# Where a token tile is transposed in the long sequence's first pass of an encoder layer

## The chip, the cores and the metric

The kernel runs on one core of a Trainium2 chip. The metric is the device time of one execution in microseconds (us). A core has five engines that run side by side, each with its own queue in order: TensorE (PE, matmuls and transposes), VectorE (DVE), ScalarE (ACT), GpSimd (POOL) and SyncE (SP, which here only issues DMAs).

## The reference

One layer of an encoder over two sequences, a short one of 512 tokens (`x_sample`) and a long one of 1024 (`x_prompt`), both of width 1024, and a final norm:

```
xn = RMSNorm(x)
z  = xn @ W_in  -> [q_A | k_A | v_A | q_B | k_B | v_B | gate_A | gate_B]
branch A: grouped-query attention (8 heads, 2 key/value heads of 64),
          q and k RMS-normalised per head, 2-D rotary
branch B: neighbourhood attention, 8 heads
mix = (sigmoid(gate_A) * (o_A @ W_pA) + sigmoid(gate_B) * (o_B @ W_pB)) @ W_out
x = x + mix
x = x + relu(RMSNorm(x) @ W_up)^2 @ W_down
```

All arrays are float32.

## The kernel before

Every float32 operand of a matmul is held as a high part (`fp32r`, written by ACT as a rounding copy) and a low part (written by DVE as source minus high part), and every product is three matmuls, high by high, high by low and low by high (`mm3`, lines 191 to 193). The short sequence goes through the token mixer first (`Trunk(0, ...)`), then the long one (`Trunk(1, ...)`); the two-matrix part of both sequences follows at the end.

`run` is the token mixer of one sequence. Its first loop, `for g in range(2)`, goes over the two key/value groups of branch A; within it `for tt in range(NT)` goes over the tiles of 128 tokens, 8 of them for the long sequence. The pass with `g == 0` is called the first pass here. In its step `tt` PE computes

- `z`, the tile's 384 columns of q, k and v (24 matmuls of 128x384, an accumulation over the 1024 rows of `W_in`),
- `values(tt - 2)`, 256 columns of branch B's values for the tile two steps back (24 matmuls of 128x256, `zvs`),
- `heads_t(tt - 2)`, three transposes of that tile's normed and rotated heads (`pqs`).

All of them read the normed tile transposed, so that the width lies along the partitions. Such a tile is made in four steps. `stat` squares the loaded tile `xt` on ACT and gets its root mean square by way of DVE (`ms_s`) and POOL (`rs_s`, a power); `scale` multiplies on DVE by that and by the norm's weights (`xns`, line 378); `p0_t` calls `transpose_tile`, which transposes the eight 128x128 blocks on PE into a PSUM tile of two banks (`ptxs`, line 275; there are two such buffers, `pbig`, shared with `pqs`), copies its halves on ACT into the high part (`xs_1h`, line 285) and subtracts them on DVE for the low part (`xs_1l`, line 291). Of the long sequence, tiles 0 to 3 are transposed while the short sequence is being finished (`ready` is then 4, and so is `r0`); tiles 4 to 7 are loaded, normed and transposed in the first pass itself (`fresh and not first`). `xs_1h` and `xs_1l` are the transposed tiles 4 to 7.

After `z` of a tile come its head norm and rotation: five squares on ACT (`sqs`), the mean on DVE (`ms_As`), the power on POOL (`rs_As`, line 176), five scalings on DVE (`ts`, line 657), two products on POOL (`us`) and the rest on DVE. DVE's queue stands still between `ms_As` and `ts` unless something is put between them.

The order on each engine is made at build time: a scheduler takes the instructions by their estimated readiness, except those passed to `tc.keep_in_program_order`, which keep the order in which the code is written among each other. `transpose_tile` pins its ACT copies and DVE subtractions if `pin` is set; before, this holds for no tile of the long sequence. In the code before, step `tt` calls `next_tile`, the transpose of tile `tt + 1`, ahead of `z`:

```
to_come = fresh and tr.ready <= tt + 1 < NT
in_z = first and to_come and tt > 0
if to_come and not in_z:
    next_tile()
```

Squares of tiles 4, 5, 6 and 7 (`stat`) are written at the end of steps 0, 1, 3 and 4, the scaling in the next step, between `ms_As` and `ts`. Normed tiles 4 and 6 share a buffer, and 5 and 7; the loaded tiles have two buffers as well, and the load of tile 6 or 7 waits until tile 4 or 5 is scaled.

Of the kernel before, what the change touches and what calls it, by code (L numbers as in the profile page):

```python
# [21 lines left out]
HD = 64  # L22
# [39 lines left out]
def encoder(ctx: ExitStack, tc: tile.TileContext, xs, outs, w):  # L62
# [107 lines left out]
    def rstd(ss, n, width, name, pin=False):  # L170
        m = sml.tile([P, 8], F32, tag="ms", name=f"ms_{name}")
        op = nc.vector.tensor_scalar(m[:, :n], ss, 1.0 / width, EPS, op0=ALU.mult, op1=ALU.add)  # L172
        if pin:
            tc.keep_in_program_order(op)
        r = sml.tile([P, 8], F32, tag="rs", name=f"rs_{name}")
        nc.gpsimd.tensor_tensor(r[:, :n], m[:, :n], mhalf[:, :n], op=ALU.pow)  # L176
        return r
# [93 lines left out]
    def transpose_tile(xn, dest, j, nm, pin=False, between=()):  # L271

        pt = big(f"pt{nm}")
        for c in range(NC8):
            nc.tensor.transpose(pt[:, c * P : (c + 1) * P], xn[:, c * P : (c + 1) * P], ident)
        view = [
            (
                pt[:, q * 512 : (q + 1) * 512].rearrange("p (c t) -> p c t", t=P),
                dest[0][q][:, :, j * P : (j + 1) * P],
                dest[1][q][:, :, j * P : (j + 1) * P],  # L280
            )
            for q in range(2)
        ]
        for src, hi, lo in view:
            op = nc.scalar.activation(hi, src, AF.Copy)
            if pin:
                tc.keep_in_program_order(op)
        for i, (src, hi, lo) in enumerate(view):
            for step in between[i : i + 1]:
                step()  # L290
            op = nc.vector.tensor_tensor(lo, src, hi.bitcast(F32), op=ALU.subtract)
            if pin:
                tc.keep_in_program_order(op)
# [57 lines left out]
    class Trunk:  # L351
# [27 lines left out]
            tc.keep_in_program_order(op)  # L379
            return xn  # L380

        def p0_t(self, tt, xn, between=()):
            tb, j = divmod(tt, 4)
            if tb not in self.xhl:
                self.xhl[tb] = new_hl(f"x{self.N}_{tb}", (True, self.NB == 1 or tb == 1))
            transpose_tile(xn, self.xhl[tb], j, f"x{self.N}_{tt}", self.t0 + tt < 4, between)
            self.ready = tt + 1

        def xh(self, tb, c):
# [5 lines left out]
    def run(tr, nxt, first):  # L395
        N, x, T, NT, NB = tr.N, tr.x, tr.T, tr.NT, tr.NB
# [85 lines left out]
        for g in range(2):  # L482
            with phase(f"phR{N}_{g}") as ph:
                xn_of = {}
                fresh = g == 0 and tr.ready < NT
                if fresh and not first:
# [10 lines left out]
                    gb = gb[:, 0]  # L497
# [108 lines left out]
                for tt in range(NT):  # L606
# [5 lines left out]
                            xn_of[3] = tr.scale(st_of.pop(3), gb)  # L612
                        flush_heads()

                    to_come = fresh and tr.ready <= tt + 1 < NT
                    in_z = first and to_come and tt > 0
                    if to_come and not in_z:
                        next_tile()
# [27 lines left out]
                    ss = sml.tile([P, 8], F32, tag="ss", name=f"ssA{nm}")  # L646
                    for i in range(5):
                        nc.scalar.activation(sq[:, i, :], zq[:, i, :], AF.Square, accum_out=ss[:, i : i + 1])
                    r = rstd(ss[:, :5], 5, HD, f"A{nm}", fresh and (tt < 2 if first else bool(st_of)))
                    ahead_ = fresh and not first and bool(st_of)  # L650
                    for t_ in list(st_of) if ahead_ else []:
                        xn_of[t_] = tr.scale(st_of.pop(t_), gb)

                    def rotate(tt, nm, z, zq, r, rt, pin):
                        t = ph.tile([P, 5, HD], F32, tag="t", name=f"t{nm}", bufs=2)
# [27 lines left out]
                    heads.append(partial(rotate, tt, nm, z, zq, r, rt, first and fresh and tt < 2 or ahead_))  # L683
                    if not (first and fresh and tt < 2):
                        flush_heads()
                    t_ = {0: 4, 1: 5, 3: 6, 4: 7}.get(tt, NT) if fresh and not first else NT
                    if t_ < NT:
                        xn = xn_to.pop(t_, None)
                        if xn is None:
                            xn = ph.tile([P, D], F32, tag=f"xn{5 - t_ & 1}", name=f"xn{N}_{t_}", bufs=1)  # L690
                        st_of[t_] = tr.stat(t_, ph, xt_of.pop(t_), xn=xn)
# [1114 lines left out]
```

## Time and profile before

| | |
|---|---|
| median of 3 runs | 2143.0 us (2142.17 to 2143.53) |
| the profiled execution | 2141.17 us |
| its span, first to last instruction | 2139.3 us |
| PE busy | 2117.0 us, 99% of the span |
| DVE busy | 1472.7 us, 69% |
| ACT busy | 1115.0 us, 52% |
| POOL busy | 390.1 us, 18% |
| mean granted clock of TensorE | 0.998 of full speed |

The profile is of one execution. Its views used here are: the page with its totals; the waits (who waited for whom, in total and at longest); windows (busy time of each engine, granted clock and DMA load in a stretch that is chosen); and the timeline (each instruction with its start, its duration, and in brackets the idle time ahead of it and what ended it). A matmul's start and end overlap those of its neighbours, since PE works on several in a row; the distance from start to start is what a matmul costs. Times are counted from the start of the span. The first pass of the long sequence lies between 379 and 451 us.

### The profile page before, as it was taken

The page shows a single profiled execution, that of the slowest core. Times are in us where ns is not written, and L with a number is a line of the kernel's source. Part 1 is how long each engine was busy: PE and PEld are TensorE (multiplying, and loading weights), DVE is VectorE, ACT ScalarE, POOL GpSimd, SP SyncE. Part 2 cuts the span into 40 slices and gives each one's busy share as a digit, 9 for nine tenths or more (in the row PEclk, how much of TensorE's full clock was granted, in tenths as well). Part 3 has the DMA queues.
Part 4 walks back from the last instruction along what each step waited for, and adds up shares of the span by engine and source line. Part 5 has one row for each costly group of instructions (what it writes and reads, how often), then busy time and mean ns, then how long its engine had stood idle before and what let it go on. Part 6 is the DMA issues. An engine that isn't in the chain of part 4 may idle for free.

```text
span 2139.3 us, 31783 instructions
## 1 busy us (share of the span) xinstructions
PE 2117.0 (99%) x10970; PEld 1849.2 (86%) x10970; DVE 1472.7 (69%) x2802; ACT 1115.0 (52%) x2343; POOL 390.1 (18%) x506
## 2 busy tenths in 40 slices
PE   9999999999999999999999999999999999999998
PEld 8888878988898888888888999999999988888886
DVE  6675686777667754656782877778777777769563
ACT  5664564557546644655530666556655643434352
POOL 2232420433233214433300200003000000000000
PEclk9999999999999999999999999999999999999999
DMA  6435567620222132433462665578544799688561
GB/s 192 125 107 168 157 185 243 191 70 26 61 77 66 43 103 85 127 104 100 148 234 105 219 194 190 166 252 206 161 144 157 261 350 342 215 287 276 159 204 62
DMA packets 319578, 350.91 MB, mean 164 GB/s; under 512 B 31160, under 2 KB 255032, under 8 KB 319417
## 3 DMA queue, kind: packets, MB, share of 16 engines
q1 hardware_dynamic: 277927, 279.65, 41.5%
q10 hardware_dynamic: 35810, 52.19, 7.0%
q0 software_dynamic: 5680, 17.04, 2.9%
q8 instruction: 87, 1.43, 0.3%
q14 instruction: 74, 0.61, 0.1%
HBM read 264.85 MB, written 87.88 MB: 165 GB/s over the span
## 4 chain that ended last, share of the span: by engine, by line
PE 51%; DVE 1%; issue 0%; ACT 0%; POOL 0%; POOLq 0%; DVEq 0%
PE dn L191 6%; PE dn L193 6%; PE dn L192 6%; PE ud L192 2%; PE uc L192 2%; PE uc L191 2%; PE ud L191 2%; PE ud L193 2%; PE uc L193 2%; PE ua L192 2%; PE ua L191 2%; PE ua L193 2%; PE ops L191 1%; PE ops L192 1%; PE ops L193 1%; PE ub L192 1%
## 5 line engine op out<-in xcount | busy, mean ns | idle before, releaser
L193 PE MATMUL dn<-wd,al 128*128 128x512 f32 x624 | 242.8, 389 | 0.0
L192 PE MATMUL dn<-wd,ah 128*128 128x512 f32 x624 | 242.8, 389 | 0.0
L191 PE MATMUL dn<-wd,ah 128*128 128x512 f32 x624 | 242.7, 389 | 0.0
L1274 ACT ACTIVATE ah<-ar 128x512 fp32r<-128x512 f32 x168 | 104.7, 628 | 208.9 <-PE dn L192 190.9
L1275 DVE TENSOR_TENSOR al<-ar,ah 128x512 fp32r<-128x512 f32 x168 | 115.6, 694 | 75.3 <-ACT ah L1274 66.5
L193 PEld LDWEIGHTS dn<-wd,al 128*128 128x128 f32 x624 | 117.1, 188 | 24.5
L192 PEld LDWEIGHTS dn<-wd,ah 128*128 128x128 f32 x624 | 117.1, 188 | 24.2
L191 PEld LDWEIGHTS dn<-wd,ah 128*128 128x128 f32 x624 | 117.1, 188 | 24.2
L730 POOL TENSOR_SCALAR ps<-ps,rls 128x1024 f32<-128x1024 f32 (+1 forms) x96 | 96.8, 1009 | 215.5 <-DVE rls L729 201.2
L770 DVE TENSOR_TENSOR ptls<-pTs,pths 128x512 fp32r<-128x512 f32 x160 | 107.6, 686 | 37.8 <-ACT pths L769 37.1
L769 ACT ACTIVATE pths<-pTs 128x512 fp32r<-128x512 f32 x160 | 94.1, 598 | 74.0 <-PE pTs L764 71.8
L724 DVE TENSOR_REDUCE nms<-ss 128x1 f32<-128x1024 f32 (+1 forms) x96 | 99.9, 1041 | 25.5 <-PE ss L722 25.0
L176 POOL TENSOR_TENSOR rs_f<-ms_f,mhalf 128x1 f32<-128x1 f32 x6 | 4.0, 667 | 590.7 <-DVE ms_f L172 590.7
L191 PE MATMUL gpss<-xs_0h,w_gs 128*128 128x512 f32 x256 | 104.7, 409 | 0.3
L727 ACT ACTIVATE ps<-ss,nms 128x1024 f32<-128x1024 f32 (+1 forms) x96 | 93.2, 972 | 22.5 <-DVE nms L724 20.0
L764 PEld LDWEIGHTS pTs<-ident,ps 128*128 128x128 f32 x640 | 78.1, 140 | 28.3 <-POOL ps L730 4.2
L193 PE MATMUL gpss<-xs_0h,w_gs 128*128 128x512 f32 x256 | 100.9, 394 | 0.0
L192 PE MATMUL gpss<-xs_0l,w_gs 128*128 128x512 f32 x256 | 100.8, 394 | 0.0
L764 PE MATMUL pTs<-ident,ps 128*128 128x128 f32 x640 | 98.9, 274 | 1.3 <-DVE ptls L770 0.6
L1274 ACT ACTIVATE A<-S 128x512 fp32r<-128x512 f32 x128 | 76.1, 624 | 30.5 <-DVE S L1337 26.5
L1275 DVE TENSOR_TENSOR A<-S,A 128x512 fp32r<-128x512 f32 x128 | 84.5, 686 | 3.4 <-ACT A L1274 3.4
L1393 ACT ACTIVATE c<-c 128x384 f32<-128x384 f32 x97 | 50.8, 524 | 68.0 <-DVE c L1392 67.9
(332 smaller groups left out, 6400.6 us busy)
## 6 DMA issues: line engine op xcount, KB each, us to landing
ar<-ud SPq DMA_DIRECT2D x120, 512.0 KB
br<-in_w_mlp_down_dram SPq DMA_DIRECT2D x72, 512.0 KB
rawu<-in_w_mlp_up_dram SPq DMA_DIRECT2D x64, 512.0 KB
ud<-c ACTq DMA_DIRECT2D x128, 192.0 KB
raw_gs<-in_w_in_dram SPq DMA_DIRECT2D x32, 512.0 KB
zgs<-sgs ACTq DMA_DIRECT2D x48, 256.0 KB
ud<-cs SPq DMA_DIRECT2D x64, 192.0 KB
raw_os<-in_w_out_dram SPq DMA_DIRECT2D x16, 512.0 KB
```

The lines of the kernel that those rows point to most:

```text
L191: nc.tensor.matmul(out, ah, bh, start=start, stop=False, **kw)
L192: nc.tensor.matmul(out, ah, bl, start=False, stop=False, **kw)
L193: nc.tensor.matmul(out, al, bh, start=False, stop=stop, **kw)
L724: nc.vector.tensor_reduce(nm_, s, axis=AX.X, op=ALU.max, negate=True)
L727: nc.scalar.activation(p, s, AF.Exp, bias=nm_, accum_out=l)
L730: nc.gpsimd.tensor_scalar(p, p, rl, 1.0, op0=ALU.mult, op1=ALU.mult)
L764: nc.tensor.transpose(pt[:, j * P : (j + 1) * P], PP[u, j][:, kc * P : (kc + 1) * P], ident)
L769: nc.scalar.activation(hi, pt, AF.Copy)
L770: nc.vector.tensor_tensor(lo, pt, hi.bitcast(F32), op=ALU.subtract)
L1274: nc.scalar.activation(hi, src, AF.Copy)
L1275: nc.vector.tensor_tensor(lo, src, hi.bitcast(F32), op=ALU.subtract)
L1393: nc.scalar.activation(t, t, AF.Relu)
```

## The change

Three things change in the first pass of the long sequence, and nothing else:

- The transposes are no longer written ahead of `z` of the step before their tile. In step `tt`, between the mean of the head norm (`ms_As`) and its scalings (`ts`), the code now first transposes whatever tile was scaled in the step before, and then scales the next one. Tile 4 is transposed in step 2, tile 7 in step 5.
- The copies and subtractions of these transposes are pinned in program order, so that on DVE the low part of a tile comes behind `ms_As` and in front of the next tile's scaling.
- The squares of tiles 4, 5, 6, 7 are at the end of steps 0, 1, 2, 3 (before: 0, 1, 3, 4).

No matmul, copy, subtraction or load is added or removed.

```
-        def p0_t(self, tt, xn, between=()):
+        def p0_t(self, tt, xn, between=(), pin=False):
...
-            transpose_tile(xn, self.xhl[tb], j, f"x{self.N}_{tt}", self.t0 + tt < 4, between)
+            transpose_tile(xn, self.xhl[tb], j, f"x{self.N}_{tt}", pin or self.t0 + tt < 4, between)
...
-                    to_come = fresh and tr.ready <= tt + 1 < NT
+                    to_come = fresh and first and tr.ready <= tt + 1 < NT
...
-                    r = rstd(ss[:, :5], 5, HD, f"A{nm}", fresh and (tt < 2 if first else bool(st_of)))
-                    ahead_ = fresh and not first and bool(st_of)
-                    for t_ in list(st_of) if ahead_ else []:
-                        xn_of[t_] = tr.scale(st_of.pop(t_), gb)
+                    ahead_ = fresh and not first and bool(st_of or xn_of)
+                    r = rstd(ss[:, :5], 5, HD, f"A{nm}", fresh and tt < 2 if first else ahead_)
+                    if ahead_:
+                        for t_ in list(xn_of):
+                            tr.p0_t(t_, xn_of.pop(t_), pin=True)
+                        for t_ in list(st_of):
+                            xn_of[t_] = tr.scale(st_of.pop(t_), gb)
...
-                    t_ = {0: 4, 1: 5, 3: 6, 4: 7}.get(tt, NT) if fresh and not first else NT
-                    if t_ < NT:
+                    t_ = r0 + tt
+                    if fresh and not first and t_ < NT:
```

In the orders that follow, `xs_1h` and `xs_1l` are the high and low part of the transposed tiles 4 to 7, `zs_0_4` the product `z` of tile 4, `ptxs_5` the PSUM tile into which tile 5 is transposed, `xns_5` its normed tile, and the last number of a name only counts allocations. On all engines together, the order differs from step 2 to step 6 of this pass and nowhere else; the order of DMAs on SP is the same.

DVE's queue in step 2, from the head norm's mean on, before:

```order
L172 TENSOR_SCALAR ms_As_0_2_4656<-ssAs_0_2_4650 128x5
L378 SCALAR_TENSOR_TENSOR xns_5_4416<-xts_5_4420,rs_s_5_4580,gbs_4424 128x1024
L657 SCALAR_TENSOR_TENSOR ts_0_2_4661<-zs_0_2_4586,rs_As_0_2_4658,gtab 128x64 x5
L291 TENSOR_TENSOR xs_1l_4678<-ptxs_4_4680,xs_1h_4676 128x4x128
L663 TENSOR_TENSOR vhls_0_4462<-zs_0_2_4586,vhls_0_4462 128x64
L677 TENSOR_TENSOR ts_0_2_4661<-ts_0_2_4661,rts_0_2_4584 128x320
L291 TENSOR_TENSOR xs_1l_4679<-ptxs_4_4680,xs_1h_4677 128x4x128
```

There the low part of tile 4 stands behind the scaling of tile 5 and behind the head scalings, which wait for POOL. DVE's queue at the same place with the change:

```order
L172 TENSOR_SCALAR ms_As_0_2_4656<-ssAs_0_2_4650 128x5
L291 TENSOR_TENSOR xs_1l_4662<-ptxs_4_4664,xs_1h_4660 128x4x128
L291 TENSOR_TENSOR xs_1l_4663<-ptxs_4_4664,xs_1h_4661 128x4x128
L378 SCALAR_TENSOR_TENSOR xns_5_4416<-xts_5_4420,rs_s_5_4580,gbs_4424 128x1024
L660 SCALAR_TENSOR_TENSOR ts_0_2_4678<-zs_0_2_4586,rs_As_0_2_4658,gtab 128x64 x5
L172 TENSOR_SCALAR ms_s_6_4696<-sss_6_4694 128x1
```

Both halves of the low part have moved ahead of the scaling of tile 5, which now comes two subtractions later.

PE's queue within `z` of tile 4 (step 4), around the transposes of tile 5, before:

```order
L191 MATMUL zs_0_4_4809<-wghs_0_0_4426,xs_1h_4676 128x384
L275 MATMUL ptxs_5_4794<-ident,xns_5_4416 128x128 x8
L192 MATMUL zs_0_4_4809<-wgls_0_0_4427,xs_1h_4676 128x384
L193 MATMUL zs_0_4_4809<-wghs_0_0_4426,xs_1l_4678 128x384
L191 MATMUL zs_0_4_4809<-wghs_0_1_4430,xs_1h_4677 128x384
```

The transposes stand behind the tenth of the 24 matmuls of `z`. The same with the change, from the head transposes ahead of `z` on:

```order
L573 MATMUL pqs_0_1_4758<-ident,rrs_0_1_4573 128x128 x3
L191 MATMUL zs_0_4_4817<-wghs_0_0_4426,xs_1h_4660 128x384
L192 MATMUL zs_0_4_4817<-wgls_0_0_4427,xs_1h_4660 128x384
L193 MATMUL zs_0_4_4817<-wghs_0_0_4426,xs_1l_4662 128x384
L191 MATMUL zs_0_4_4817<-wghs_0_0_4426,xs_1h_4660 128x384
L275 MATMUL ptxs_5_4779<-ident,xns_5_4416 128x128 x8
```

They now stand behind the fourth.

PE's queue around the transposes of tile 6, within `z` of tile 5, before:

```order
L192 MATMUL zs_0_5_4922<-wgls_0_1_4431,xs_1h_4677 128x384
L275 MATMUL ptxs_6_4907<-ident,xns_6_4787 128x128 x8
L193 MATMUL zs_0_5_4922<-wghs_0_1_4430,xs_1l_4679 128x384
L191 MATMUL zs_0_5_4922<-wghs_0_1_4430,xs_1h_4677 128x384
L192 MATMUL zs_0_5_4922<-wgls_0_1_4431,xs_1h_4677 128x384
```

They stand behind the twentieth matmul. With the change:

```order
L573 MATMUL pqs_0_2_4871<-ident,rrs_0_2_4690 128x128 x3
L275 MATMUL ptxs_6_4892<-ident,xns_6_4693 128x128 x8
L191 MATMUL zs_0_5_4923<-wghs_0_0_4426,xs_1h_4660 128x384
L192 MATMUL zs_0_5_4923<-wgls_0_0_4427,xs_1h_4660 128x384
L193 MATMUL zs_0_5_4923<-wghs_0_0_4426,xs_1l_4662 128x384
```

They now come ahead of the whole of `z`, right behind the head transposes, and tile 7 moves in the same way, to the front of `z` of tile 6. On ACT, the squares of tile 6 move ahead of the squares of `z` of tile 3 and of the copies of `values(1)` and `heads_t(1)`, right behind the copy of tile 4's high part, and the copy of `z` 2's values (`vhls`) moves between the two halves of tile 5's high part.

## The prediction

> **What bounds the kernel now.** I read the page's totals first, then who PE waited for, then the stretch of the changed pass in windows, then each engine's timeline in it.
>
> ```profile
> span 2139.3 us, 31783 instructions
> ...
> PE 2117.0 (99%) x10970; PEld 1849.2 (86%) x10970; DVE 1472.7 (69%) x2802; ACT 1115.0 (52%) x2343; POOL 390.1 (18%) x506
> ```
>
> PE is busy for 99% of the span, and only 22.3 us of it are not. The change adds and removes no work, so all it can win is PE's idle time, and time in which PE runs slowly. The waits of PE over the whole span say where that is (times waited for in total, how often, longest):
>
> ```profile
> PE zs L193 <- DVE xs_1l L291: 2.1, 1, 2.1
> ...
> PE ptxs L275 <- DVE xns L378: 0.4, 2, 0.2
> ```
>
> The longest wait of PE anywhere is the first row: a matmul of `z` waits once for the low part of a transposed tile. That, and the two short waits for a normed tile, are what the change touches. The windows of this pass (columns: busy time of PE, weight loads, DVE, ACT, POOL; then the granted clock, DMA share, GB/s):
>
> ```profile
> 403.40:406.90 3.50, 1.36 (x8) 1.04 (x7) 1.97 (x8) 1.77 (x7) 2.12 (x3) 1.00 0.53 150
> 406.90:410.40 3.50, 3.50 (x15) 3.32 (x15) 3.44 (x10) 0.39 (x1) 0.83 (x2) 0.52 0.27 94
> ...
> 415.65:424.30 8.65, 8.47 (x62) 8.18 (x61) 5.82 (x17) 3.56 (x18) 4.39 (x5) 1.00 0.31 93
> 424.31:432.97 8.66, 8.48 (x63) 8.19 (x61) 6.09 (x17) 3.59 (x18) 3.88 (x4) 1.00 0.11 38
> ```
>
> In the first row PE is idle for 2.14 of 3.50 us; in the next 3.50 us its granted clock is 0.52. So the wait is paid twice: once as a wait, and once as a slow stretch that costs 0.48 x 3.50 = 1.7 us. The last two rows are the two following steps, at full clock, with DVE 70% busy: nothing but PE is short there.
>
> PE's timeline gives the price of each piece of a step (start, duration, idle time in brackets):
>
> ```profile
> 398.18 0.49 PE L573 MATMUL pqs<-ident,rrs 128*128 128x128 f32 x3
> 398.51 1.04 PE L275 MATMUL ptxs<-ident,xns 128*128 128x128 f32 x8
> 399.30 0.42 PE L192 MATMUL zs<-wgls,xs_0h 128*128 128x384 f32 x1
> ...
> 403.37 0.42 PE L191 MATMUL zs<-wghs,xs_1h 128*128 128x384 f32 x1
> 403.63 0.34 PE L192 MATMUL zs<-wgls,xs_1h 128*128 128x384 f32 x1
> 406.10 0.44 PE L193 MATMUL zs<-wghs,xs_1l 128*128 128x384 f32 x1 [2.14 <-DVE xs_1l L291]
> 406.38 0.33 PE L191 MATMUL zs<-wghs,xs_1h 128*128 128x384 f32 x1
> 406.55 0.34 PE L192 MATMUL zs<-wgls,xs_1h 128*128 128x384 f32 x1
> ...
> 415.40 0.49 PE L573 MATMUL pqs<-ident,rrs 128*128 128x128 f32 x3
> 415.65 0.42 PE L191 MATMUL zs<-wghs,xs_1h 128*128 128x384 f32 x1
> ...
> 428.24 1.06 PE L275 MATMUL ptxs<-ident,xns 128*128 128x128 f32 x8 [0.18 <-DVE xns L378]
> ...
> 432.97 0.42 PE L191 MATMUL zs<-wghs,xs_1h 128*128 128x384 f32 x1
> ...
> 440.08 0.49 PE L573 MATMUL pqs<-ident,rrs 128*128 128x128 f32 x3
> ```
>
> A step without transposes of a tile: `z` and `values` take 440.08 - 432.97 = 7.11 us, `pqs` 415.65 - 415.40 = 0.25. Transposes right behind `pqs` add (399.30 - 398.18) - 0.25 = 0.87. An undisturbed step with a transpose is then 7.11 + 0.25 + 0.87 = 8.23 us. Measured are 415.65 - 403.37 = 12.28 us for the step of tile 4, that is 4.05 too much, and (432.97 - 415.65) / 2 = 8.66 for those of tiles 5 and 6, 0.43 too much each. At most 4.05 + 0.86 = 4.91 us are to be had in this pass.
>
> **The change part by part.** *Low part in front of the scaling (DVE).*
>
> ```profile
> 401.96 0.17 DVE L172 TENSOR_SCALAR ms_As<-ssAs 128x5 f32<-128x5 f32 x1
> 402.05 1.28 DVE L378 SCALAR_TENSOR_TENSOR xns<-xts,rs_s,gbs 128x1024 f32<-128x1024 f32 x1
> 404.40 1.05 DVE L657 SCALAR_TENSOR_TENSOR ts<-zs,rs_As,gtab 128x64 f32<-128x64 f32 x5 [1.08 <-POOL rs_As L176]
> 405.37 0.68 DVE L291 TENSOR_TENSOR xs_1l<-ptxs,xs_1h 128x512 fp32r<-128x512 f32 x1
> ...
> 409.64 0.17 DVE L172 TENSOR_SCALAR ms_As<-ssAs 128x5 f32<-128x5 f32 x1
> ...
> 423.77 1.28 DVE L291 TENSOR_TENSOR xs_1l<-ptxs,xs_1h 128x512 fp32r<-128x512 f32 x2
> 424.97 0.41 DVE L600 TENSOR_TENSOR vts<-zvs,vts 128x256 fp32r<-128x256 f32 x1
> 426.81 1.28 DVE L378 SCALAR_TENSOR_TENSOR xns<-xts,rs_s,gbs 128x1024 f32<-128x1024 f32 x1
> ```
>
> DVE was at `ms_As` at 401.96, then scaled tile 5, stood 1.08 us for POOL, and reached the first half of the low part at 405.37; it ended at 406.05, and PE went on at 406.10. Its source was long there:
>
> ```profile
> 400.73 1.08 ACT L285 ACTIVATE xs_1h<-ptxs 128x512 fp32r<-128x512 f32 x2
> ...
> 402.66 1.11 ACT L371 ACTIVATE xns<-xts 128x1024 f32<-128x1024 f32 x1
> ```
>
> ACT has copied both halves by 401.81. With the change the first half starts at 402.05 and ends at 402.73, the second at 402.65 + 0.68 = 403.33. PE asks for the first at 403.63 + 0.17 = 403.80 (0.17 is the distance 406.55 - 406.38). So the 2.14 us go, and with them, as I read the windows, the 1.7 us at half clock.
>
> *Scaling of tile 5 behind the low part.* Two subtractions take 424.97 - 423.77 = 1.20 us, so the scaling starts at 403.25 instead of 402.05, and here POOL comes in:
>
> ```profile
> 402.22 2.15 POOL L176 TENSOR_TENSOR rs_As<-ms_As,mhalf 128x5 f32<-128x5 f32 x1 [1.28 <-DVE ms_As L172]
> ...
> 405.53 1.15 POOL L671 TENSOR_TENSOR us<-ts,rts 128x160 f32<-128x160 f32 x2 [1.17 <-DVE ts L657]
> ...
> 433.88 1.18 POOL L176 TENSOR_TENSOR rs_As<-ms_As,mhalf 128x5 f32<-128x5 f32 x1 [1.18 <-DVE ms_As L172]
> ```
>
> The same power takes 2.15 us beside a scaling and 1.18 alone, so a scaling holds POOL up; `us`, beside a subtraction from PSUM (405.37), shows no such delay. Moved behind the subtractions, the scaling meets a power that began at 402.22 and ends at 403.40. Whether DVE then waits for POOL no row shows: 0 to 0.15 us (403.25 against 403.40). I take 0.15, since the rows show that one of the two stands. [...]
>
> *Transposes of tile 5 behind the fourth matmul of `z`.* Their turn comes at 403.63 + 3 x 0.17 = 404.14. The scaled tile is there at 403.40 + 1.28 = 404.68, and PE took 428.24 - (426.81 + 1.28) = 0.15 us to start after a scaling. A new wait of 404.83 - 404.14 = 0.69 us, the only one I add. It is queued ahead of the other 20 matmuls of `z`.
>
> *Transposes of tiles 6 and 7 ahead of `z`.* PE comes to those of tile 6 at 403.37 + 7.11 + 0.87 + 0.69 + 0.25 = 412.3. On DVE the stretch from `ts` to the next `ms_As` was 409.64 - 404.40 = 5.24 us with two subtractions of 1.20 in all, which now stand elsewhere. From a `ts` at 404.6 the next `ms_As` is at 408.6 to 409.2 (the subtractions covered up to 0.6 us of a wait for `us`); two subtractions and a scaling later, 2.48 us, tile 6 is scaled at 411.1 to 411.7, and PE sees it at 411.8 at the latest. No wait, with 0.5 us to spare. The PSUM buffer (low part of tile 5 read by 410.4) is free by then. For tile 7 DVE has a step of 8.23 us for about 6 us of work (windows, last rows), so the slack grows. These steps lose their 0.43 us each.
>
> *Squares of tile 6 earlier on ACT.* They are ready to go at 401.81 instead of 402.66. Before, they started at 402.66 with no bracket, so the load was there by then; at worst ACT stands 0.85 us, with the copies of `values(1)` and `heads_t(1)` behind. Those copies feed transposes a step later and are hidden under `z` of tile 4; if that cover went, the tile's 0.5 us of slack would go first. I take 0.
>
> *Loads on SP.* The order stays. The load of tile 7 waits for the scaling of tile 5, 1.35 us later than before:
>
> ```profile
> 403.40 0.33 SPq L246 DMA_DIRECT2D xts<-in_x_prompt_dram  x1
> ```
>
> It is 0.5 MB, and 403.40:406.90 moved 150 GB/s x 3.5 us = 0.52 MB: it lands about 3.5 us after issue, at 408.3. ACT, free at about 407, stands a microsecond in front of its squares, but the next work behind them needs the end of `z` of tile 4, at 409.2. Cost 0; between 0 and 0.5.
>
> **Sum.** Step of tile 4: 12.28 - (8.23 + 0.69) = 3.36; steps of tiles 5 and 6: 2 x 0.43 = 0.86; together 4.22 us, and PE is the bound to the end, so it arrives there whole. The profiled execution took 2141.17 us, which gives 2136.95; the median of the runs is 1.83 above it, so 2138.8.
>
> **Rivals.** *The half clock stays.* The slow stretch might not come from the wait. Then 1.7 us less are gained: 2140.5. [...] Against it: the rows, with the clock at 0.52 for 3.50 us right behind the wait and at 1.00 in the steps after it. Chance 0.08.
>
> *Given back later.* PE comes to `values`, the attention's first tiles and the gate 4 us earlier; if DVE or ACT set their time, PE waits there instead. Against it: DVE 5.8 to 6.1 of 8.66 us busy. Time about 2142. Chance 0.11.
>
> *Nothing changes*, since a wait with several causes is put down to the last: then the low part was not it, and 2143. But it ends at 406.05 and PE goes on at 406.10. Chance 0.03.
>
> *Slower.* With the transposes in front, all of `z` of tiles 5 and 6 now stands behind the scaled tile, where before 20 matmuls ran first. From 0.5 us of lateness on each microsecond costs PE one, and a gap like the 2.14 one brings another 1.7 us of slow clock. Past the 4.22 gained by 0.2% it is when both tiles are some 3.1 us late, 2 x (2.6 + 1.7) = 8.6: 2147.4. The bounds on DVE and on the loads above are far from that. Chance 0.06.
>
> **How the numbers follow.** A difference of 0.2%, 4.3 us, is about what can be told from none. My own case has 0.72, with 3.6 to 4.9 gained (2138.1 to 2139.4), and its sum lies on that bound: 0.40 of it faster, 0.32 the same. The same further has 0.08 + 0.11 + 0.03, so 0.54; slower 0.06. The range goes up to 2142.0, which leaves out the slower case, the unchanged one and half of the gain given back, and down to 2137.2, below the most that the pass can give, for what the runs scatter.
>
> **What would show it.** Right: no wait of PE for `xs_1l`; granted clock 1.00 throughout 402 to 412; PE waits for `xns` once, 0.5 to 0.8 us, at about 404; POOL's `rs_As` near 1.2 us and no idle DVE in front of `ts`; `z` of tile 7 starting at 428.7 instead of 432.97. Wrong: transposes of tile 6 or 7 with a bracket; a slow stretch without a long wait; waits of PE after 440 that were not there before.

## The result, and the profile after

| | before | after |
|---|---|---|
| median of 22 runs each | 2141.2 us (2140.2 to 2143.53) | 2138.35 us (2137.78 to 2141.43) |
| ratio, 95% interval | | 0.9987 (0.9982 to 0.9993) |
| the profiled execution | 2141.17 us | 2138.32 us |

The change wins 2.85 us, 0.13%, in the medians and in the two profiled executions alike. The prediction had 4.22 from the same profiled execution. The page's totals after:

```profile
span 2136.5 us, 31789 instructions
...
PE 2115.7 (99%) x10970; PEld 1848.4 (87%) x10970; DVE 1471.4 (69%) x2802; ACT 1116.4 (52%) x2343; POOL 389.1 (18%) x506
```

The windows of the changed pass (columns as in the prediction):

```profile
403.40:406.90 3.50, 3.02 (x22) 2.73 (x21) 3.06 (x11) 3.04 (x15) 1.21 (x4) 1.00 0.31 72
406.90:410.40 3.50, 3.50 (x25) 3.50 (x24) 3.34 (x9) 2.27 (x12) 2.04 (x4) 1.00 0.46 172
412.40:420.00 7.60, 7.60 (x55) 7.60 (x54) 6.59 (x18) 3.46 (x17) 3.61 (x5) 1.00 0.12 43
420.00:429.00 9.00, 9.00 (x68) 9.00 (x67) 6.66 (x21) 4.12 (x19) 4.45 (x7) 1.00 0.32 97
```

PE was idle for 2.14 us in the first of them and is now idle for 0.48; the clock of 0.52 behind it is 1.00; in the steps of tiles 5 and 6 PE does not pause. PE's timeline of the pass:

```profile
403.43 0.42 PE L191 MATMUL zs<-wghs,xs_1h 128*128 128x384 f32 x1
...
404.86 1.06 PE L275 MATMUL ptxs<-ident,xns 128*128 128x128 f32 x8 [0.48 <-DVE xns L378]
...
412.45 1.04 PE L275 MATMUL ptxs<-ident,xns 128*128 128x128 f32 x8
...
420.69 1.04 PE L275 MATMUL ptxs<-ident,xns 128*128 128x128 f32 x8
...
428.85 0.42 PE L191 MATMUL zs<-wghs,xs_1h 128*128 128x384 f32 x1
```

`z` of tile 4 starts 0.06 us later than before (403.43 against 403.37), `z` of tile 7 4.12 us earlier (428.85 against 432.97). So the pass itself gained 4.18 us, 25.42 instead of 29.60, of a predicted 4.22. DVE and POOL within it:

```profile
402.02 0.17 DVE L172 TENSOR_SCALAR ms_As<-ssAs 128x5 f32<-128x5 f32 x1
402.23 1.29 DVE L291 TENSOR_TENSOR xs_1l<-ptxs,xs_1h 128x512 fp32r<-128x512 f32 x2
403.44 1.27 DVE L378 SCALAR_TENSOR_TENSOR xns<-xts,rs_s,gbs 128x1024 f32<-128x1024 f32 x1
404.63 1.04 DVE L660 SCALAR_TENSOR_TENSOR ts<-zs,rs_As,gtab 128x64 f32<-128x64 f32 x5
```

```profile
402.28 1.18 POOL L176 TENSOR_TENSOR rs_As<-ms_As,mhalf 128x5 f32<-128x5 f32 x1 [1.27 <-DVE ms_As L172]
```

DVE has no bracket from the mean to the head scalings any more, and the power takes 1.18 us instead of 2.15.

The end of the program is only 2.82 us earlier, so 1.30 us of the 4.12 were given back behind the pass. Where, is read by following one PE instruction after another in both traces. First at the attention's second tile; before, then after:

```profile
451.78 0.50 PE L721 MATMUL ss<-kTs,qTs 128*128 128x512 f32 x1 [0.22 <-ACT kTs L577]
```

```profile
448.14 0.50 PE L724 MATMUL ss<-kTs,qTs 128*128 128x512 f32 x1 [0.69 <-ACT kTs L577]
```

PE waits 0.47 us longer there for the transposed key of tile 7, and its lead over before falls from 4.12 to 3.64, and to 3.54 within the next 5 us. Its origin lies 15 us earlier on DVE, at tile 6; before, then after:

```profile
437.75 0.49 DVE L677 TENSOR_TENSOR ts<-ts,rts 128x320 f32<-128x320 f32 x1
438.28 0.49 DVE L679 TENSOR_TENSOR rrs<-ts,us 128x320 f32<-128x320 f32 x1
438.69 3.82 DVE L186 TENSOR_TENSOR w_gs<-raw_gs,w_gs 128x512 fp32r<-128x512 f32 x6
442.44 0.16 DVE L172 TENSOR_SCALAR ms_As<-ssAs 128x5 f32<-128x5 f32 x1
```

```profile
433.18 0.49 DVE L680 TENSOR_TENSOR ts<-ts,rts 128x320 f32<-128x320 f32 x1 [0.76 <-POOL us L674]
433.59 0.28 DVE L580 TENSOR_TENSOR kTs<-pqs,kTs 128x128 fp32r<-128x128 f32 x1
433.88 0.86 DVE L582 TENSOR_TENSOR qTs<-pqs,qTs 64x256 fp32r<-64x256 f32 x2
434.77 0.49 DVE L682 TENSOR_TENSOR rrs<-ts,us 128x320 f32<-128x320 f32 x1
435.18 3.69 DVE L186 TENSOR_TENSOR w_gs<-raw_gs,w_gs 128x512 fp32r<-128x512 f32 x6
438.80 0.16 DVE L172 TENSOR_SCALAR ms_As<-ssAs 128x5 f32<-128x5 f32 x1
```

Before, the subtractions of the heads filled DVE's time until POOL's product was there; now DVE stands 0.76 us for it and does them afterwards. From `ts` to `rrs` its lead falls from 4.57 to 3.51, a packed queue (`w_gs`) carries that to the mean of tile 7's head norm, and so to the key that PE waits for.

Two more losses lie 500 us further on, in branch B. POOL's product `os_Bs`, before and after, and DVE's subtraction for a weight beside it:

```profile
948.96 0.72 POOL L1013 TENSOR_TENSOR os_Bs<-os_Bs 64x256 f32<-64x256 f32 x1
948.99 1.25 DVE L186 TENSOR_TENSOR w_bks<-raw_bks,w_bks 128x512 fp32r<-128x512 f32 x1 [0.21 <-ACT w_bks L180]
```

```profile
945.39 1.18 POOL L1016 TENSOR_TENSOR os_Bs<-os_Bs 64x256 f32<-64x256 f32 x1
945.13 0.84 DVE L186 TENSOR_TENSOR w_bks<-raw_bks,w_bks 128x512 fp32r<-128x512 f32 x1
```

In these rows the one that began second took longer. Before it was DVE (1.25 us; the same subtraction took 0.67 at 950.71, where it began ahead of POOL); now DVE begins 0.26 us ahead of POOL's product and POOL pays (1.18 against 0.72), and PE's lead falls by 0.22 (3.57 to 3.35). Then, at 959:

```profile
959.34 0.56 DVE L938 CUSTOM_DVE_ANT_0 sbss<-sbs,bms 128x384 f32<-128x384 f32 x1 [1.22 <-issue]
```

```profile
956.35 0.56 DVE L941 CUSTOM_DVE_ANT_0 sbss<-sbs,bms 128x384 f32<-128x384 f32 x1 [1.57 <-issue]
```

The `sbs` that it reads starts on PE at 958.69 before and 955.34 after, so DVE begins 0.65 us behind it before and 1.01 us after, with a cause that no engine shows ("issue"); the lead falls from 3.34 to 2.99. With 0.14 won back at 1000 to 1050 and 0.30 lost at 1215 to 1230, where two profiles of the kernel before already differ by 0.21, 2.82 us arrive.

### The profile page after: what moved, and what is told of

It reads as the page before. It is cut to its first block, busy times and chain, and to the rows that moved or that the text cites. A ratio compares the mean times of both kernels' runs of the same rounds, so it can differ in the third digit from the quotient of the medians.

```text
span 2136.5 us, 31789 instructions
## 1 busy us (share of the span) xinstructions
PE 2115.7 (99%) x10970; PEld 1848.4 (87%) x10970; DVE 1471.4 (69%) x2802; ACT 1116.4 (52%) x2343; POOL 389.1 (18%) x506
## 4 chain that ended last, share of the span: by engine, by line
PE 51%; DVE 1%; issue 0%; ACT 0%; POOL 0%; POOLq 0%; DVEq 0%
PE dn L191 6%; PE dn L193 6%; PE dn L192 6%; PE uc L191 2%; PE uc L192 2%; PE ud L192 2%; PE ud L191 2%; PE ud L193 2%; PE uc L193 2%; PE ua L192 2%; PE ua L191 2%; PE ua L193 2%; PE ops L193 1%; PE ops L191 1%; PE ops L192 1%; PE ub L192 1%
```

## The experiments

The theory after the comparison: the wait and the half clock left with the move of the low part, and 1.3 us fell to three places where PE does not set the time. The rivals: the pass gains by something else (the order against the scaling, the earlier squares); the half clock has another cause than the wait; the losses behind the pass are scatter and not caused by the order. The timed kernels had 11 runs each; "one run" is a single execution.

**Both kernels once more.**

> The kernel before, unchanged, profiled a second time, to see what repeats. Theory (the pass loses 4.05 us at tile 4 in every execution): PE waits 2.1 us for xs_1l at tile 4, granted clock near 0.5 in the 3.5 us behind it, first score matmul of the attention's first tile about 48.4 us after the start of z of tile 4. Rival (the stretch at half clock is the throttle's own accident): wait of 2.1 us again, but clock 1.00 behind it, and the first score matmul 1.7 us earlier. For the later places: if the waits of PE for msbs at 950 to 960 us differ by 0.3 us or more from those of the first profile, differences of that size between two kernels there say nothing.

> The changed kernel, unchanged, profiled a second time and timed once more. Theory: 4.1 to 4.2 us gained at the start of z of tile 7, 3.6 at the first score matmul, where PE waits 0.7 us for kTs again, and 2.5 to 3.2 us in the whole (ratio 0.9985 to 0.9988). Rival (the 1.4 us that were given back are scatter of one profile): the wait for kTs is 0.2 us this time, and the gain of the whole 4 us (0.9981).

Before, 2141.93 us (one run): the wait of 2.14 us for `xs_1l` is there again, with the clock at 0.50 behind it. After, 2138.9 (ratio 0.9987, 0.9978 to 0.9996): the wait for `kTs` is 0.64, and the losses at 945 and 959 are in the same places. So the losses repeat from one execution to the next. The one at 959 is not this order's alone: the kernel of before with eight more matmuls, further below, has it too.

**Scaling first, low part behind it.**

```
 if ahead_:
+    done = list(xn_of)
     for t_ in list(st_of):
         xn_of[t_] = tr.scale(st_of.pop(t_), gb)
+    for t_ in done:
+        tr.p0_t(t_, xn_of.pop(t_), pin=True)
```

> The changed kernel, but with the next tile scaled ahead of the low part of the present one, in all three steps. Theory A (what gained is that the low part is no longer behind DVE's wait for the power; its place against the scaling matters by a scaling's 1.28 us and no more): scaling 401.9 to 403.2, low part's first half done by about 403.9 against 403.80 wanted, so PE waits for xs_1l 0.1 to 0.35 us, not at all for xns of tile 5, clock 1.00; POOL's rs_As takes 2.1 us again but ends at 404.4, under the low part; time from 0.3 us below that of the changed kernel to the same. Rival B (the low part has to stand in front of the scaling): PE waits 1 us or more for xs_1l, a slow stretch behind it, and 2 to 4 us of the gain are lost.

2138.43 us (0.9986, 0.9977 to 0.9995), no different from after, and in the pass a gain of 4.18 again. DVE, and POOL beside it:

```profile
404.60 1.28 DVE L378 SCALAR_TENSOR_TENSOR xns<-xts,rs_s,gbs 128x1024 f32<-128x1024 f32 x1
405.91 1.29 DVE L291 TENSOR_TENSOR xs_1l<-ptxs,xs_1h 128x512 fp32r<-128x512 f32 x2
407.11 0.47 DVE L661 SCALAR_TENSOR_TENSOR ts<-zs,rs_As,gtab 128x64 f32<-128x64 f32 x2
```

```profile
404.77 2.15 POOL L176 TENSOR_TENSOR rs_As<-ms_As,mhalf 128x5 f32<-128x5 f32 x1 [1.28 <-DVE ms_As L172]
```

The power takes 2.15 us again, 0.17 us behind the scaling, but now the low part covers it. PE's wait for `xs_1l` is then 0.14 us in its bracket, and about 0.3 by the distance of the starts around it; that for the scaled tile falls to 0.07. So "in front of the scaling" is worth nothing by itself; what counts is that the low part stands in front of `ts`, where DVE waited.

**The squares alone, and the transposes alone.** The first is the kernel before with the earlier squares, the second the kernel after with the old ones:

```
# squares alone                       # transposes alone
-    t_ = {0: 4, 1: 5, 3: 6, 4: 7}...  -    t_ = r0 + tt
+    t_ = r0 + tt if fresh and ...     +    t_ = {0: 4, 1: 5, 3: 6, 4: 7}...
```

> The kernel before with one part of the change alone: the squares of tiles 6 and 7 a step earlier; the transposes keep their place in the code and nothing is pinned. The scheduler then puts the transposes of tiles 6 and 7 in front of z, as in the changed kernel, and leaves those of tile 5 and the low part of tile 4 (behind the scaling and the head scalings) where they were. Theory (the two parts add): the 2.14 us wait and the slow stretch stay, 2 x 0.43 = 0.86 us are gained, time 0.5 to 0.9 us below before, ratio 0.9996 to 0.9998. Rival (it is the early squares and transposes that free DVE for the low part): the wait shrinks to under 1.5 us and 2 us or more are gained, ratio 0.9990 or less.

> The changed kernel without its third part: the squares of tiles 6 and 7 again in steps 3 and 4. The low part of tiles 4 and 5 stands in front of the next scaling as in the change, but tile 6 is now transposed right ahead of its own z, and tile 7 as well. Theory (the low part can only stand in DVE's wait if the tile is scaled a step earlier, so the parts don't add): no wait at tile 4, clock 1.00 there; but PE waits for the high or low part of tile 6, and again of tile 7, 1.5 to 3 us each, and the gain of 4.2 us at z of tile 7 is gone or turned round; ratio 0.9995 to 1.0020. Rival (the parts add): 0.4 us per tile is lost, ratio 0.9991.

Neither half gains: 2142.47 us (1.0002, 0.9993 to 1.0011) and 2143.12 (1.0007, 0.9998 to 1.0015). With the squares alone PE waits where it did, and at tiles 6 and 7 in addition:

```profile
407.54 0.45 PE L193 MATMUL zs<-wghs,xs_1l 128*128 128x384 f32 x1 [2.18 <-DVE xs_1l L291]
...
417.03 1.06 PE L275 MATMUL ptxs<-ident,xns 128*128 128x128 f32 x8 [0.97 <-DVE xs_1l L291]
```

With the transposes alone the wait at tile 4 is gone and the clock stays at 1.00, but PE then stands in front of the next tiles, not for the low part, as was expected, but for the heads ahead of the transposes:

```profile
423.66 0.41 PE L573 MATMUL pqs<-ident,rrs 128*128 128x128 f32 x2 [2.62 <-DVE qTs L582]
...
433.68 0.41 PE L573 MATMUL pqs<-ident,rrs 128*128 128x128 f32 x2 [1.59 <-DVE qTs L582]
```

The parts do not add. The scaled tile must be ready earlier if it stands ahead of all of `z`, and only the earlier squares make it so. That the effects could be summed was expected of the squares alone, and fell there; for the transposes alone it was expected that they can't, which held, though by another wait than the one named.

**The wait put back, in two sizes.** DVE does 2 or 4 reductions between the low part and the scaling of tile 5, and the fifth matmul of `z` is kept behind the transposes of tile 5, so that PE waits for the scaled tile:

```
     tr.p0_t(t_, xn_of.pop(t_), pin=True)
+for _ in range(2 if tt == 2 else 0):          # 4 in the other kernel
+    scr = sml.tile([P, 1], F32, tag="nm", name=f"scr{nm}_{_}")
+    op = nc.vector.tensor_reduce(scr, gb[:, 0:512], axis=AX.X, op=ALU.max, negate=True)
+    tc.keep_in_program_order(op)
```

> The changed kernel with PE's order held and two idle reductions of 128x512 put on DVE in step 2, between the low part of tile 4 and the scaling of tile 5 (extra work, nothing left out). At 0.6 us each (a subtraction of that width takes 0.60 in the profile after) PE's one wait for xns of tile 5 grows from 0.48 to about 1.7 us. What it asks: which length of wait is followed by the slow stretch that stood behind the 2.14 us wait of the kernel before. Theory A (the slow stretch is the price of a wait of about 2 us, and a shorter one is free of it): granted clock 1.00 in the 3.5 us behind the wait, z of tile 7 starts 1.2 us later than in the kernel changed. Theory B (any wait from somewhat over 1 us on brings it): clock near 0.5, z of tile 7 starts 2.9 us later. Rival C (the slow stretch had nothing to do with the wait): clock 1.00 here and in the next run.

> The same with four idle reductions: PE's wait for xns of tile 5 grows to about 2.9 us. Theories A and B: granted clock 0.5 to 0.6 in the 3.5 us behind the wait, and z of tile 7 starts 2.4 us (the longer wait) and 1.7 us (the slow stretch) later than in the changed kernel, 4.1 us in all. Rival C: clock 1.00, z of tile 7 starts 2.4 us later.

One run each: 2138.97 us and 2142.44. PE in the first kernel:

```profile
405.89 1.07 PE L284 MATMUL ptxs<-ident,xns 128*128 128x128 f32 x8 [1.67 <-DVE xns L387]
```

PE in the second, and the windows ahead of the wait's end and behind it:

```profile
407.53 1.49 PE L284 MATMUL ptxs<-ident,xns 128*128 128x128 f32 x6 [2.86 <-DVE xns L387]
```

```profile
404.14:407.55 3.41, 0.55 (x5) 0.26 (x3) 3.41 (x7) 1.65 (x11) 0.00 (x0) 1.00 0.00 0
407.55:410.96 3.41, 3.41 (x14) 3.41 (x15) 2.08 (x11) 1.21 (x3) 1.68 (x4) 0.50 0.64 200
```

A wait of 1.67 leaves the clock at 1.00, and `z` of tile 7 comes 1.19 us later than after, counted from `z` of tile 4 on (1.67 - 0.48). A wait of 2.86 brings 3.41 us at half clock, and `z` of tile 7 comes 4.0 us later: 2.38 for the longer wait (2.86 - 0.48) and 1.7 for the slow stretch. The slow stretch follows the wait, and here it cost what the prediction had put on it.

**When the clock falls.** In the profiles together the half-clock stretches within the program are all 3.41 us long (the one at its end lasts until the end), and where one execution has two, their edges lie a whole number of 3.4133 us apart (with eight more matmuls, below: 279.36 and 409.05, 38 of them; before: 407.05 and 2134.2, 506 of them, from which the 3.4133 is worked out). Cut in such steps, a step is in all profiles but one at 0.50 where weight loads filled 1.47 us or less of the step before it (0.26 with four reductions, 1.47 with the scaling first), and at 1.00 from 1.49 up (the last kernel below); only steps that begin in the first 5 us of the program stand apart (1.10 to 1.39 us of loads, and 1.00 behind them). Before, cut so:

```profile
403.64:407.05 3.41, 1.27 (x7) 0.95 (x7) 2.12 (x8) 1.53 (x7) 1.88 (x3) 1.00 0.54 154
407.05:410.47 3.42, 3.42 (x16) 3.24 (x15) 3.36 (x10) 0.46 (x1) 0.90 (x2) 0.50 0.27 96
```

The one that does not fit is the kernel with the rotation on DVE alone, described last. Its step at 276 us holds only 1.30 us of weight loads, and the step behind it is at 1.00 all the same:

```profile
275.81:279.22 3.41, 2.04 (x11) 1.30 (x9) 3.27 (x8) 3.26 (x6) 0.00 (x0) 1.00 0.46 130
```

So the edges fit the steps, but 1.47 us of loads is only what parted the other profiles, not a rule.

So it would matter whether the wait of 2.14 us lies in one step or across an edge. To shift the pass against the steps, the kernel before got 3 or 8 more matmuls of the short sequence's projection, long ahead:

```
+if first and c == 3 and k == 0:
+    for i_ in range(8):                         # 3 in the control
+        nc.tensor.matmul(pp_of[tb], wp[k][0], mv[0], start=True, stop=True)
```

> The kernel before with three idle matmuls of 128x512 in the short sequence's projection, at about 330 us; the order of PE in the changed pass stays, all of it comes 0.7 us later. In the profiles so far each stretch at half clock is 3.4 us long and all their edges in one profile lie on a grid of 3.413 us (407.05 and 2134.2 in the kernel before are 506 steps apart); a step was slow if weight loads filled less than 1.45 us of the step ahead of it, and not from 1.6 us on. Theory D (the clock is judged in steps of this grid, so a wait of 2.14 us brings the slow stretch only where it falls into one step): the wait of 2.14 us began 0.3 and 0.5 us behind an edge in the two profiles of before; 0.7 us later it still lies within one step, so the slow stretch stays and z of tile 7 starts about 0.7 us later than in before. Rival (the wait alone decides): the same. This run is the control for the next.

> The same with eight idle matmuls, 1.84 us of work added to PE and nothing taken away. Theory D: the wait of 2.14 us for xs_1l stays, but now lies across an edge of the grid, with about 1.2 us of it on either side; the granted clock stays 1.00 in the 3.5 us behind it, so z of tile 7 starts 0.1 us later than in before (1.84 added, 1.7 saved), and the time is that of before within 0.5 us (ratio 0.9998 to 1.0002). Rival (a wait of over 2 us brings the slow stretch wherever it lies): clock 0.5 behind the wait, z of tile 7 and the whole 1.8 us later (ratio 1.0008). If the granted clock falls at 280 us in this execution, as it did in three of the profiles, all behind it shifts by another 1.7 us, and the two swap places; then the edges of that profile decide.

The control: 2142.94 us (one run), wait 2.14, half clock from 408.05 to 411.5, as before. With eight matmuls the time was 2144.32 (1.0011, 1.0002 to 1.002), above what was expected; the eight put the start of the pass off by 2.23 us in the later profile below, and in the first profile the clock also fell at 279.36, which moved the pass again. There the wait lay almost whole in one step:

```profile
405.64:409.05 3.41, 1.34 (x11) 1.02 (x9) 2.34 (x8) 1.80 (x8) 2.25 (x2) 1.00 0.47 127
409.05:412.46 3.41, 3.35 (x11) 3.25 (x12) 2.85 (x9) 0.74 (x3) 0.96 (x3) 0.50 0.15 51
```

That run fitted the steps but did not tell them from a rule by the length of the wait, so the same kernel was profiled again:

> The kernel of the run before with eight idle matmuls, profiled a second time. In its first profile the clock had also fallen at 280 us, and the wait lay within one step of the grid again, 2.07 of its 2.13 us. What is asked: whether the step that holds the wait says if the clock falls. Theory D, made sharper by all steps of eleven profiles: the clock falls to 0.50 for the next 3.41 us if weight loads filled at most 1.47 us of the step, and not from 1.49 us on; so if the clock does not fall at 280 us, the wait of 2.1 us lies across an edge, 1.6 to 2.2 us of weight loads stand in each of the two steps, and the granted clock stays 1.00 behind it; if it falls at 280 us again, it falls behind the wait again. Rival (a wait of over 2 us brings it wherever it lies): clock 0.50 behind the wait in either case.

2143.48 us (one run). Now the wait lies across an edge, at 407.29. PE, then the two steps and their clock:

```profile
408.33 0.44 PE L193 MATMUL zs<-wghs,xs_1l 128*128 128x384 f32 x1 [2.13 <-DVE xs_1l L291]
```

```profile
403.88:407.29 3.41, 2.32 (x19) 2.00 (x17) 2.30 (x7) 2.23 (x13) 2.15 (x1) 1.00 0.27 67
407.29:410.71 3.42, 2.18 (x13) 1.89 (x14) 2.88 (x10) 1.30 (x5) 1.48 (x3) 1.00 0.36 139
```

The same wait of 2.13 us, in the same place of the program, and no fall of the clock. It did not fall either behind the 2.18 us wait of the squares-alone kernel, nor behind the 2.62 us of the transposes alone, which also lie across an edge (406.36 and 422.46): the mean granted clock is 0.998 in the one, with its fall at 280.07, and 0.999 in the other. So length alone does not decide. And the old pass at full clock takes 28.94 us instead of 29.60: the slow stretch was worth only 0.66 us there, since at full clock PE comes earlier to the transposes of tile 6 and waits 0.74 us for them.

Both profiles of this kernel also bear on the loss at 959. Its order on DVE is that of before from 340 us on, and yet DVE begins that `sbss` 1.01 us behind PE's `sbs` (961.18 against 960.17 in the later profile), as in after, and not 0.65 as in before. So this loss of 0.35 us can come with a mere shift in time, without the change.

**The rotation of tile 6 behind the heads, on DVE alone and with ACT and branch B.** Edges of order that make no engine wait for another:

```
-nc.vector.tensor_tensor(t, t, rt[:, 0:1, :]...)
+op = nc.vector.tensor_tensor(t, t, rt[:, 0:1, :]...)
+behind(op, tt)          # tile 6: behind the last subtraction of heads_t(4)
 # the same for the subtraction vhl; in the second kernel also
 # ACT's copy vhl, behind the copies of heads_t(4), and in branch B
 # DVE's first piece of w_bk behind the second sbs of unit (4, (0,))
```

> The changed kernel, with one thing on DVE moved: at tile 6 the subtractions for kTs and qTs of tile 4 stand ahead of vhls and of the product ts, as they did before the change (where they covered DVE's wait for POOL's us). Theory (this order gives back 0.5 us at the start of the attention): DVE's wait of 0.76 us in front of rrs goes, PE's wait for kTs falls from 0.7 to about 0.2 us, first score matmul 4.1 us earlier than before instead of 3.6, the whole 0.3 to 0.5 us below the changed kernel. Rival (another chain, on ACT or POOL, sets that time): the wait for kTs stays 0.6 to 0.7 us and the time is that of the changed kernel.

> The changed kernel with two places mended at which its gain is given back. (1) At tile 6 the copies and subtractions for kTs and qTs of tile 4 stand ahead of vhls, on ACT as well as on DVE (the run called tail moved DVE's alone, and DVE then waited 0.78 us for ACT's copy, which stood behind vhls). (2) In branch B one subtraction for w_bks (two operands in SBUF, on DVE) stands behind the next sbss instead of ahead of it, so that POOL's sum os_Bs is no longer under way together with a subtraction that began first (1.18 us there after the change, 0.72 before). Theory: (1) the first score matmul waits 0.1 to 0.3 us for kTs instead of 0.7, 0.4 to 0.6 us gained; (2) os_Bs takes 0.72 to 0.75, and the 0.56 us that the changed kernel loses against before between 945 and 966 us do not appear; together the shift at the end is 3.6 to 4.0 us against before, time 0.8 to 1.1 us below the changed kernel. Rival to (1): another link (ACT's weight copies) sets the time of kTs and the wait stays 0.6 or more. Rival to (2): the 0.56 us come from elsewhere and are lost again with os_Bs at 0.72.

On DVE alone: 2138.57 us (0.9986, 0.9977 to 0.9995), and the theory behind it fell. DVE's wait only changed its name:

```profile
432.54 0.29 DVE L590 TENSOR_TENSOR kTs<-pqs,kTs 128x128 fp32r<-128x128 f32 x1 [0.78 <-ACT qTs L589]
```

ACT's copies for `kTs` and `qTs` stood behind its copy `vhls`, so ACT was late instead. With ACT reordered too, DVE, and PE at the attention's second tile:

```profile
434.02 0.28 DVE L600 TENSOR_TENSOR kTs<-pqs,kTs 128x128 fp32r<-128x128 f32 x1
...
435.34 0.48 DVE L702 TENSOR_TENSOR ts<-ts,rts 128x320 f32<-128x320 f32 x1
```

```profile
449.35 0.50 PE L747 MATMUL ss<-kTs,qTs 128*128 128x512 f32 x1
```

No wait is left on either, and of 4.13 us at `z` of tile 7 all is still there behind the attention's start (4.22; after: 4.18 fell to 3.59). That loss is shown to be DVE's and ACT's order at tile 6. In branch B POOL's product is back at its short time, and DVE pays:

```profile
946.73 0.72 POOL L1041 TENSOR_TENSOR os_Bs<-os_Bs 64x256 f32<-64x256 f32 x1
```

```profile
946.97 1.91 DVE L188 TENSOR_TENSOR w_bks<-raw_bks,w_bks 128x512 fp32r<-128x512 f32 x1
```

The loss there falls from 0.22 to 0.04 us; that at 959 stays (0.35). From the start of its pass to the end this kernel keeps 3.79 us, where after keeps 2.88. Its median is 2138.37 (0.9984, 0.9975 to 0.9992), no better than after's as it stands.

Why not, the clock of the runs tells in part. Each run records its mean granted clock to three places. The profiled executions whose only half-clock stretch is that at the program's end have 0.999, those with one more 0.998, the one with two more 0.997. Beside the fall in the changed pass there is one at 280 us, in the short sequence's branch B, which four profiles show, whatever the change: squares alone (280.07), the one with eight matmuls (279.36), scaling first (280.54), and this one (280.44), each 3.41 us at 0.50 or 0.51, which is 1.7 us by the author's estimate if PE sets the time all through (3.41 x 0.5). Among runs at 0.999 the last kernel has 2137.44 (7 runs), after 2138.34 (26 runs of two sets), before 2141.03 (28 runs of the sets behind the first, which agree within 0.2 us): the last gains 0.9 us on after, with an interval of 1.33 less to 0.11 more, so the gain is likely and not shown.

## Why the prediction came out as it did

The forecast of 2138.8 us lies 0.45 from the median, on a sum that had two errors of opposite sign; that it lies so near is partly luck. One is in its base: it stands on a median of three runs, 2143.0, and 22 runs of the same kernel have 2141.2, 1.8 less. The other is the gain, 4.22 forecast and 2.85 measured, 1.4 too much, nearly all of it given back behind the pass.

- *The step of tile 4* (12.28 to 8.92, a gain of 3.36) *and those of tiles 5 and 6* (0.86): right. From head transposes to head transposes the three steps now take 8.95, 8.24 and 8.23 us, worked out 8.92, 8.23 and 8.23. The only new wait, for the scaled tile of step 4, puts the transposes off by 0.65 us by the distance of the starts (404.86 against 404.04 + 0.17), where 0.69 was worked out; its bracket says 0.48, since it counts from the end of the matmul ahead; the transposes of tiles 6 and 7 have no bracket.
- *0.15 us for DVE held by POOL*: not seen. The power ended at 403.46 and the scaling began at 403.44, behind its predecessor without a bracket; the low part started 0.21 us behind the mean, not 0.09, which took the same time. The 0.15 was an estimate from the edges of two rows, and no run shows it. That no row shows whether DVE waits for POOL was wrong: in the trace of before, at 948.99, DVE's subtraction for `w_bks` takes 1.25 us beside a POOL product that began 0.03 us ahead, and 0.67 at 950.71.
- *"The wait is paid twice", 1.7 us at half clock*: right that it comes from the wait, by the two sizes of wait, and right as a price where PE is the bound behind it, as in the kernel with four reductions. As a share of this gain it was mis-sized: in the old order the stretch cost 0.66, since without it PE waits at tile 6. The sum did not suffer, since it was made from whole steps, measured against the price of an undisturbed one. The rival *the half clock stays* did not come about: the clock is 1.00 at 406.90 to 410.40 now that the wait is gone. But the fall came behind a wait of 2.14 us here and not behind one of 2.62 us elsewhere, so the length of a wait alone does not decide.
- *"PE is the bound to the end, so it arrives there whole"*: this is the step that failed. 4.12 us were ahead at `z` of tile 7 and 2.82 arrived. PE's 99% is a mean, and it says nothing on the few places where it waits anyway: the row for `kTs` with 0.22 us stood in the timeline of before, and a wait that is there already grows when all ahead of it gets faster. The rival *given back later* named the mechanism for the attention's first tiles, and at 0.58 it was right there, but it priced it all or nothing. The losses at 945 and 959 are not of that kind, since nothing is moved there. At 945 the changed timing let DVE and POOL meet in another order; at 959 the cause is open.
- *ACT a microsecond in front of the squares of tile 7*: 1.23 us, and harmless, as worked out.
- *What would prove it wrong, "waits of PE after 440 that were not there before"*: it came true in the small: the wait for `kTs` grew from 0.22 to 0.69.

Runs at the same clock give the change a gain of 2.70 us (2.43 to 2.93). By the traces it would be 4.18 - 0.66 - 1.30 = 2.2, or 2.5 if the 0.30 at 1215 us is scatter. The medians of all runs lie little further apart, 2.85: of before 42 of 70 runs were below 0.999, of after 7 of 33, and the 37 of before at 0.998 lie only 0.70 us above those at 0.999.

Open: why DVE begins 0.35 us later at 959; why ACT's copy ahead of 945 runs 0.28 us earlier against PE, though its order is the same; and how many of the runs at 0.998 had their fall at 280 us and how many in the pass.

## What to carry to other kernels

Make the sum from the distance between two instructions of the bounding engine, ahead of the change and behind it, against an undisturbed step, and not from waits and slow clock as items of their own, since a time saved uncovers the wait behind it. Then walk on from there to the next places where that engine waits for another, however short the wait: a gain of microseconds is cut by the slack of each, and moving work on one engine alone often just hands the wait to the next. Two parts of an edit that gain nothing apart may gain together, as here, so a trial of one half says little on the whole.

## What the runs showed of the hardware

- In the profiles of this case the granted clock fell to 0.50 within the program for 3.41 us at a time (before 407.05:410.47, with four reductions 407.55:410.96, with eight more matmuls 279.36:282.77 and 409.05:412.46). Where one execution had two falls, their edges lay a whole number of 3.413 us apart (38 and 506 of them), and the place of these steps differed from one execution to the next (an edge at 409.05 in the first profile with eight matmuls, at 407.29 in the second). Cut so, and past the first 5 us, the step ahead of a fall held 1.47 us of weight loads or less (0.26 with four reductions, 404.14:407.55; 1.47 with the scaling first, 277.12:280.54), and every other step 1.49 us or more (the least in the last kernel, 2127.05:2130.46), but for one of 1.30 us in the kernel with the rotation on DVE alone (275.81:279.22). PE's busy time did not part the two: behind 1.75 us the clock stayed at 1.00 (two reductions, 404.05:407.46), behind 2.08 us it fell (squares alone, 276.66:280.07). A fall also came behind several short waits in one step: at 279.36, with eight matmuls, behind waits of 0.41, 0.41 and 0.66 us. The same kernel had the fall in one execution and not in the next (eight matmuls: 0.50 from 409.05, and 1.00 from 407.29). What exactly is counted stays open; no run tested it by itself.
- In some rows DVE or POOL took longer where both were at work: POOL's product `os_Bs` 0.72 us in before (948.96) and 1.18 in after (945.39, DVE 0.26 us ahead); POOL's power 1.18 in after (402.28), and 2.15 where it began 0.17 us behind a scaling, in before (402.22) and with the scaling first (404.77); DVE's subtraction for `w_bks` 0.67 in before (950.71), 1.25 in before (948.99, POOL 0.03 us ahead) and 1.91 with ACT and branch B reordered (946.97, POOL 0.24 us ahead). In these rows the slower one had begun second; why was not tested.
- DVE started 0.35 us later at one place (959) in after, its second profile and three of the orders derived from it (scaling first, and the two with the rotation behind the heads), and not in the kernels with two or four more DVE instructions ahead (0.65 us behind PE there again). It did so too in both profiles of before with eight more matmuls (1.01 us behind PE, as in after), and not with three. So neither DVE's order nor the number of its instructions decides it alone; the cause was not found.
